# Four paddings in SBUF that shift the operands of the large matmuls to multiples of 512 bytes

## The chip, the cores and the metric

The kernel runs on one core of one Trainium2 chip. The metric is device time in microseconds (us) of one execution; the runs of a kernel are given as a median.

## The reference, cut to what matters

One layer of an encoder over 512 tokens of 1024 channels, all in float32:

```python
h = rms_norm(x, norm_mix_pre)
za, zb, q, k, v, su, sv, gl = split(h @ w_in)            # 1024 x 10240
a = silu(layer_norm(depthwise_conv(za * sigmoid(zb))))   # 31 taps
y_a = a @ w_proj_conv
o = rms_norm(diff_attention(q, k, v)) * (1 - lam_init)   # 8 heads, two softmaxes each
y_b = o @ w_proj_attn
y_c = spatial_gating(gelu(su), layer_norm(gelu(sv))) @ w_proj_sgu
g_a, g_b, g_c = split(sigmoid(gl + b_gate))
x = x + rms_norm((g_a * y_a + g_b * y_b + g_c * y_c) @ w_out)
f = square(relu(rms_norm(x) @ w_ffn_up)) @ w_ffn_down    # 1024 x 4096, 4096 x 1024
out = x + rms_norm(f)
```

## The kernel before, in words

**The products.** Every large product is made in float32r from split operands: each side has a high part (`hh`, `w_hi`, `bh`, ...) and a low part (`hl`, `w_lo`, `bl`, ...), and `mm3` (L221) issues three matmuls per K-tile of 128, high x high, low x high and high x low, into one PSUM bank. All go through `pe.matmul` at L57, all transposes through L61, both kept in the order of the program; so the trace has one line for all matmuls and they are told apart by their tiles.

```python
def mm3(o, s, m, first, last):                              # L221
    pe.matmul(o, s[0], m[0], start=first, stop=False)
    pe.matmul(o, s[0], m[1], start=False, stop=False)
    pe.matmul(o, s[1], m[0], start=False, stop=last)
```

A matmul has a stationary operand, 128 columns (512 bytes per partition) loaded by an LDWEIGHTS of its own before each matmul, and a moving operand, 512 columns (2048 bytes) or 256. A *unit* (`unit_gen`, L227) is one weight tile of 128 columns against all of K = 1024 and all 512 tokens: 24 matmuls, weights stationary, tokens moving. In this form are the units on h (the GLU's za and zb, q, k, su, the gates gl: 61 of them with 512 columns at a time; three more are done in halves of 256 columns at the start, beside the norm of x), the three branches' projections (8 units each) and the projection up (32 units, the first four with one half of 256 columns in advance). In the other form, token tile stationary and 512 columns of weights moving, are sv (192 matmuls, `sv_half`), w_out (192, `out_mm`) and the projection down (768, `down_mm`); v has it with 256 columns (384 matmuls). The attention adds scores (128), products with v (96) and transposes.

**Weights.** `load_to` (L134) loads each 512 KB weight tile by a DMA on SP's queue into `w_raw`, ScalarE rounds it to `w_hi` (L145) and VectorE takes the rest to `w_lo` (L146); three buffers of each. Five tiles, from the second half of w_out on (`xp`, L122), go into buffers of the pool `p4`.

**Other engines.** VectorE also has the 8 x 31 taps of the depthwise conv (L325), as work of low priority behind the GLU and the branches, and the conv branch's norm starts with transposes of `apad` on TensorE.

**Where tiles lie.** SBUF is handed out by pools that stand on each other like a stack, each tile rounded up to 32 bytes per partition; a pool closed gives its place to the next one. The order is: a descriptor area of 16,384 bytes and four constants of 32; `wp` with nine weight buffers of 4096; `cp` (ident, 512 bytes, and 18 small tiles); `hp` with hh and hl of 16,384 each; `cq` with the small parameters (3680 bytes); `cvp` with apad (17,344) and acc (2048); `mixp` with mix (16,384); then, one after the other, `att`, or `brp` (bh, bl) with `sgu`, `p3` or `p4` on it. The MLP's pool `fp` (gpo, 4096; fh and fl, 65,536 each) starts where cq did. Summed up, the addresses' residues modulo 512 are:

| tiles | address of the first | residue |
|---|---|---|
| w_raw, w_hi, w_lo | 16,512 | 128 |
| hh, hl, also h2h, h2l | 54,464 | 192 |
| conv buffer apad | 90,912 | 288 |
| attention's operands; bh, bl (also sh, sl, mh, ml); gvh, gvl, ch, cl | 126,688 and up | 224 |
| w_hi, w_lo in p4 | 167,648 and up | 224 |
| fh, fl | 91,328, 156,864 | 192 |

Within a tile the operands begin at multiples of 512 bytes.

Of the kernel before, what the change touches and what calls it, by code (L numbers as in the profile page):

```python
# [8 lines left out]
F32 = mybir.dt.float32  # L9
# [4 lines left out]
PSUM = bass.MemoryType.PSUM  # L14
DRAM = bass.MemoryType.DRAM

P = 128
# [11 lines left out]
SCALE = 64 ** -0.5  # L29
# A head whose sum of squares leaves float32's range has the norm factor 0, as 1 / sqrt(inf).  # L30
# The squares are summed at a scale of 2^-40, so that the sum itself stays finite.
BIG = 2.0 ** 64
# How the work is laid beside each other: the GLU's channel tiles of each head, the units ahead of the
# first head, the taps behind a GLU tile, the gate at which the conv branch's norm starts, the places at
# which the token tiles of the second norm are turned, the load of x behind which the first weights go, and
# how far behind the taps stand.
LATE = {1: [2], 3: [3], 5: [4], 6: [5], 7: [6, 7]}
# [10 lines left out]
def encoder_layer(ctx: ExitStack, tc: tile.TileContext, a: dict, out: bass.AP):  # L48
# [3 lines left out]
    class pe:  # L52
        """The tensor engine, in the order of the program."""

# [8 lines left out]
    def mk(name, bufs=1, **kw):  # L63
        return tc.tile_pool(name=name, bufs=bufs, reuse_waits="tile", **kw)
# [7 lines left out]

    # ------------------------------------------------------------ weights
    x = a["x"]
# [6 lines left out]
    def rows(n, k0, c0):  # L81
        return wv[n][:, k0:k0 + 2, c0:c0 + 512]
# [4 lines left out]
    specs = []  # L87
    # channel tiles of the GLU that wait for the attention, whose softmax leaves the tensor engine time
    late = {h: [] for h in range(H)}
# [37 lines left out]
    for nh in range(2):  # L127
        specs += [rows("w_ffn_down", k, nh * 512) for k in range(0, FT, 2)]

    wp = ctx.enter_context(mk("wp"))  # L130
    loaded = []
# [17 lines left out]
    def take(m=1, ahead=2):  # L149
        i = taken[0]  # L150
        taken[0] += m
        load_to(i + m + ahead)
        return loaded[i:i + m]

    # ------------------------------------------------------------ constants
    cp = ctx.enter_context(mk("cp"))
    hp = ctx.enter_context(mk("hp"))
    ps = {"pool": None, "a": 4, "b": 4}

    def banks(stack, na):  # L160
        """PSUM's eight banks: na for "a", the others for "b", until the stack closes."""
        ps.update(pool=stack.enter_context(mk(f"ps{na}", space=PSUM)), a=na, b=8 - na)
# [11 lines left out]
    big = ExitStack()  # L174
# [9 lines left out]
    def eps_with(p, ss, scale):  # L184
        """eps and the part of the mean square that is there already."""
        e = p.tile([P, 1], F32, tag="rs_e", bufs=4, name="rs_e")
        vec.tensor_scalar(e, ss, scale, EPS, op0=ALU.mult, op1=ALU.add)
        return e

    def rstd_of(p, ss, scale, eps=EPS, eps_tile=None, n=1, steps=1):  # L190
        """(ss * scale + eps) ** -0.5: ScalarE's root, then Newton steps to float32's accuracy."""
        v = p.tile([P, n], F32, tag=f"rs_v{n}", bufs=4 if n == 1 else 1, name="rs_v")
        vec.tensor_scalar(v, ss, scale, eps, op0=ALU.mult, op1=ALU.add)
        s = p.tile([P, n], F32, tag=f"rs_s{n}", bufs=4 if n == 1 else 1, name="rs_s")
        act.activation(s, ss, AF.Sqrt, bias=eps_t if eps_tile is None else eps_tile, scale=scale)
        r = p.tile([P, n], F32, tag=f"rs_r{n}", bufs=4 if n == 1 else 1, name="rs_r")
        vec.reciprocal(r, s)
        for _ in range(steps):
            if n == 1:
                vec.scalar_tensor_tensor(s, v, r, r, op0=ALU.mult, op1=ALU.mult)  # L200
            else:
                vec.tensor_tensor(s, v, r, op=ALU.mult)
                vec.tensor_tensor(s, s, r, op=ALU.mult)
            vec.tensor_scalar(s, s, -0.5, 1.5, op0=ALU.mult, op1=ALU.add)
            vec.tensor_tensor(r, r, s, op=ALU.mult)
        return r
# [14 lines left out]
    def mm3(o, s, m, first, last):  # L221
        """o += s^T @ m from the parts of both: three passes, what lies under float32's last bit left out."""
        pe.matmul(o, s[0], m[0], start=first, stop=False)
        pe.matmul(o, s[0], m[1], start=False, stop=False)
        pe.matmul(o, s[1], m[0], start=False, stop=last)

    def unit_gen(b, w, mov, tk=slice(0, S)):  # L227
        """b[c, tok] = W[:, c]^T @ mov, all of K = 1024."""
        for kt in range(KT):
            mm3(b, [t[:, kt] for t in w], [t[:, kt, tk] for t in mov], kt == 0, kt == KT - 1)  # L230
            yield
# [7 lines left out]

    # ------------------------------------------------------------ h = rms_norm(x), transposed  # L240
    hh = hp.tile([P, KT, S], F32R, tag="hh", name="hh")
    hl = hp.tile([P, KT, S], F32R, tag="hl", name="hl")
    with mk("p0") as p0:
# [25 lines left out]

        # the first units run on half of the tokens while the others are normalized  # L270
        hT = (hh, hl)
        norm_x(0)
        norm_x(1)
        first = take(3, 0)
# [7 lines left out]

        # small parameters: one column per block of 128 channels
        rowsrc = [("conv_b", 8), ("conv_ln_g", 8), ("conv_ln_b", 8), ("b_gate", 24), ("subln_g", 1), ("sgu_b", 8)]
# [11 lines left out]
        b = bank("b")  # L296
# [12 lines left out]

    # ------------------------------------------------------------ conv branch: GLU, then taps in the background  # L310
    cvp = big.enter_context(mk("cvp"))
    apad = cvp.tile([P, KT, S + 2 * PAD], F32, tag="apad", name="apad")
    pool.memset(apad[:, :, 0:PAD], 0.0)
    pool.memset(apad[:, :, PAD + S:], 0.0)
    mixp = big.enter_context(mk("mixp"))

# [12 lines left out]
    taps = conv_taps()  # L329

    def conv(n, behind):
        """The next n taps, behind an instruction of VectorE: work that fills its time there."""
        with tc.issue_after(behind.ins):
            keep = tc.cur_priority
            tc.cur_priority = keep + LOWP
            for _ in range(n):
                next(taps, None)
            tc.cur_priority = keep + (tc.cur_priority - keep - LOWP)
# [24 lines left out]
    b = bank("a")  # L363
# [4 lines left out]

    # -lambda
    lam2 = []  # L370
# [13 lines left out]

    # ------------------------------------------------------------ differential attention
    dist = ap_.tile([P, 896], F32, tag="dist", bufs=2, name="dist")
# [10 lines left out]
    def proj_qk(h, got):  # L397
        """q (times -1/8) and k of one head, both of its maps, as what two passes of K = 128 need:
        [qh; qh], [ql; ql] against [kh; kl], whose products are all four of the parts'."""
        wq, wk = take(2)  # L400
        bq = bank("a")
        yield from unit_gen(bq, wq, hT)
        qh = ap_.tile([P, 2, S], F32R, tag="qh", bufs=2, name="qh")
        ql = ap_.tile([P, 2, S], F32R, tag="ql", bufs=2, name="ql")
# [33 lines left out]
    def head(h, got):  # L438
        """One head of differential attention; yields where the tensor engine would wait."""
        qh, ql, kk = got["qk", h]  # L440
# [42 lines left out]
        b = bank("b")  # L483
# [6 lines left out]
        b = bank("b")  # L490
# [13 lines left out]
    run(proj_qk(0, got))  # L504
    # beside each head's softmax: the next head's q and k, and the next pair's v or a channel tile of the GLU
    fills, quota = [], []
    for h in range(H):
        n = 0
# [33 lines left out]

    # ------------------------------------------------------------ gmlp: v half, gelu and layer norm
    sg_g = bcast(sp, "sg_g", a["sgu_ln_g"], D)
# [16 lines left out]

    # ------------------------------------------------------------ attention: rms over each head, back to channels
    oss2 = oss.rearrange("p t h -> p (t h)")
# [7 lines left out]
    for h in range(H):  # L571
        next(fill)
        next(fill)
        b = bank("a")
# [29 lines left out]

    # ------------------------------------------------------------ gate and merge one branch
    mix = mixp.tile([P, KT, S], F32, tag="mix", name="mix")
# [30 lines left out]

    # ------------------------------------------------------------ spatial gating
    ws_t = {}
# [31 lines left out]
    for g in range(KT):  # L671
        (w,) = take(1)
        gc = slice(g * P, (g + 1) * P)
        b = bank("b")
# [14 lines left out]

    # ------------------------------------------------------------ conv branch: layer norm, silu  # L690
    c3 = ExitStack()
# [39 lines left out]

    # ------------------------------------------------------------ w_out, residual, second norm
    dp = ctx.enter_context(mk("dp", space=DRAM))
# [3 lines left out]
    with mk("p4") as p4:  # L737
# [21 lines left out]
        for t in range(TT):  # L759
# [4 lines left out]
            ss = p4.tile([P, 2], F32, tag="ss", bufs=4, name="ss")  # L764
# [23 lines left out]

    # ------------------------------------------------------------ squared-relu MLP
    fp = ctx.enter_context(mk("fp"))  # L790
# [3 lines left out]
    for n in range(FT):  # L794
        if n < len(early):
            b = eb[n]
            run(unit_gen(b[:, 256:512], early[n], h2, slice(256, 512)))
        else:
            (w,) = take(1)
            b = bank("a")  # L800
# [16 lines left out]
    ss = cp.tile([P, TT, 2], F32, tag="fss", name="fss")  # L817
# [58 lines left out]
```

## Time and profile before

| | us |
|---|---|
| runs of the kernel, median (lowest to highest) | 1106.67 (1105.45 to 1106.84) |
| profiled execution, span from its first to its last instruction | 1102.8 |
| TensorE busy in it | 1081.2 |
| VectorE, ScalarE busy in it | 706.2, 497.6 |

The runs' times are those of whole executions, and the span is that of the one that was profiled, without what lies ahead of its first instruction and behind its last; the runs' median is 3.9 us more than the span, and no other time is listed for the profiled execution. Times in the trace are counted from the start of the span. A matmul's busy time in the trace is longer than the distance to the start of the next, because matmuls are pipelined and their ends are modelled.

### The profile page before, as it was taken

What the parts mean: (1) busy time and instruction counts of PE and PEld (TensorE: products, weight loads), DVE (VectorE), ACT (ScalarE), POOL (GpSimd) and SP (SyncE); (2) the same over time, 40 slices, a digit from 0 to 9 for tenths busy, and PEclk for the clock granted to TensorE, in tenths of its full rate; (3) what the DMA queues carried; (4) which work ended last, traced back from release to release, by engine and by line L of the source; (5) the groups of instructions that cost most, each with busy time, mean ns of one, the idle gap of its engine ahead of it and who ended that gap; (6) DMA issues with size and microseconds to landing.
All of it is one profiled execution on the core that took longest, in us unless ns stands there. A gap on an engine that the chain in (4) does not pass through costs nothing.

```text
span 1102.8 us, 13477 instructions
## 1 busy us (share of the span) xinstructions
PE 1081.2 (98%) x5201; PEld 897.4 (81%) x5201; DVE 706.2 (64%) x1200; ACT 497.6 (45%) x800; POOL 14.0 (1%) x32
## 2 busy tenths in 40 slices
PE   5999999999999999999999999999999999999997
PEld 4989898988878888888888888889888888888885
DVE  5686878979995888997995564485444443223224
ACT  5356667777644832443222953354333332112111
POOL 3000000000000000000000000000000000000000
PEclk9999999999999999999999999999999999999999
DMA  7242333233323333223333132832333334222222
GB/s 220 78 122 74 93 96 86 68 107 85 96 78 95 115 95 94 79 78 94 96 96 96 45 109 97 267 126 86 97 97 97 96 103 164 94 93 96 96 77 77
DMA packets 149439, 111.78 MB, mean 101 GB/s; under 512 B 3957, under 2 KB 130977, under 8 KB 149376
## 3 DMA queue, kind: packets, MB, share of 16 engines
q1 hardware_dynamic: 146368, 101.73, 30.7%
q0 software_dynamic: 2288, 7.63, 2.0%
q10 hardware_dynamic: 720, 1.57, 0.4%
q8 instruction: 41, 0.67, 0.3%
q14 instruction: 22, 0.18, 0.1%
HBM read 102.52 MB, written 4.19 MB: 97 GB/s over the span
## 4 chain that ended last, share of the span: by engine, by line
PE 94%; DVE 2%; ACT 2%; DMA 1%; issue 0%; SPq 0%; DVEq 0%; ACTq 0%
PE ps_a L57 74%; PE ps_b L57 17%; PE ps_b L61 3%; DMA w_raw<-in_w_in_dram 1%; ACT y L704 0%; DVE jk L778 0%; DVE w_lo L146 0%; PE ps_a L61 0%; ACT jk L776 0%; SPq L251 0%; ACT w_hi L145 0%; DVE wk L773 0%; DVE st L589 0%; DVE h2l L218 0%; DVE wk L772 0%
## 5 line engine op out<-in xcount | busy, mean ns | idle before, releaser
L145 ACT ACTIVATE w_hi<-w_raw 128x1024 fp32r<-128x1024 f32 x176 | 186.4, 1059 | 405.2 <-PE ps_a L57 308.5
L146 DVE TENSOR_TENSOR w_lo<-w_raw,w_hi 128x1024 fp32r<-128x1024 f32 x176 | 215.1, 1223 | 228.2 <-ACT w_hi L145 227.6
L57 PE MATMUL ps_a<-hh,w_hi 128*128 128x512 f32 (+1 forms) x536 | 209.1, 390 | 0.2 <-ACT hh L217 0.2
L57 PE MATMUL ps_a<-hl,w_hi 128*128 128x512 f32 (+1 forms) x536 | 206.7, 386 | 0.3 <-DVE hl L218 0.3
L57 PE MATMUL ps_a<-hh,w_lo 128*128 128x512 f32 (+1 forms) x536 | 205.6, 384 | 0.0
L325 DVE SCALAR_TENSOR_TENSOR acc<-apad,convw,acc 128x512 f32<-128x512 f32 x232 | 173.6, 748 | 5.1
L57 PEld LDWEIGHTS ps_a<-hh,w_lo 128*128 128x128 f32 x536 | 102.1, 191 | 20.6
L57 PEld LDWEIGHTS ps_a<-hh,w_hi 128*128 128x128 f32 x536 | 102.4, 191 | 20.1 <-ACT hh L217 0.6
L57 PEld LDWEIGHTS ps_a<-hl,w_hi 128*128 128x128 f32 x536 | 102.3, 191 | 19.4 <-DVE hl L218 0.6
L57 PE MATMUL ps_a<-h2h,w_hi 128*128 128x512 f32 (+1 forms) x288 | 106.3, 369 | 0.0
L57 PE MATMUL ps_a<-h2h,w_lo 128*128 128x512 f32 (+1 forms) x288 | 105.7, 367 | 0.0
L57 PE MATMUL ps_a<-h2l,w_hi 128*128 128x512 f32 (+1 forms) x288 | 105.0, 364 | 0.0
L57 PEld LDWEIGHTS ps_a<-h2h,w_lo 128*128 128x128 f32 x288 | 54.0, 188 | 9.8
L57 PEld LDWEIGHTS ps_a<-h2l,w_hi 128*128 128x128 f32 x288 | 54.1, 188 | 9.6 <-DVE h2l L218 0.2
L57 PEld LDWEIGHTS ps_a<-h2h,w_hi 128*128 128x128 f32 x288 | 54.1, 188 | 8.4
L57 PE MATMUL ps_a<-w_hi,fl 128*128 128x512 f32 x128 | 50.4, 394 | 0.0
L57 PE MATMUL ps_b<-w_hi,fl 128*128 128x512 f32 x128 | 50.4, 394 | 0.0
L57 PE MATMUL ps_a<-w_hi,fh 128*128 128x512 f32 x128 | 50.4, 394 | 0.0
L57 PE MATMUL ps_a<-w_lo,fh 128*128 128x512 f32 x128 | 50.4, 394 | 0.0
L57 PE MATMUL ps_b<-w_hi,fh 128*128 128x512 f32 x128 | 50.4, 394 | 0.0
L57 PE MATMUL ps_b<-w_lo,fh 128*128 128x512 f32 x128 | 50.4, 394 | 0.0
L57 PE MATMUL ps_a<-w_hi,hh 128*128 128x256 f32 (+1 forms) x160 | 49.2, 308 | 0.0
(240 smaller groups left out, 1808.8 us busy)
## 6 DMA issues: line engine op xcount, KB each, us to landing
w_raw<-in_w_in_dram SPq DMA_DIRECT2D x80, 512.0 KB, 3.6
w_raw<-in_w_ffn_up_dram SPq DMA_DIRECT2D x32, 512.0 KB, 4.0
w_raw<-in_w_ffn_down_dram SPq DMA_DIRECT2D x32, 512.0 KB, 3.5
w_raw<-in_w_proj_attn_dram SPq DMA_DIRECT2D x8, 512.0 KB, 3.9
w_raw<-in_w_proj_sgu_dram SPq DMA_DIRECT2D x8, 512.0 KB, 3.8
w_raw<-in_w_proj_conv_dram SPq DMA_DIRECT2D x8, 512.0 KB, 4.0
w_raw<-in_w_out_dram SPq DMA_DIRECT2D x8, 512.0 KB, 3.5
xx<-in_x_dram SPq DMA_DIRECT2D x4, 512.0 KB, 7.6
```

What stands on the lines that cost most here:

```text
L57: return tc.keep_in_program_order(nc.tensor.matmul(*args, **kw))
L61: return tc.keep_in_program_order(nc.tensor.transpose(*args, **kw))
L145: act.activation(hi, raw, AF.Copy)
L146: vec.tensor_tensor(lo, raw, f32(hi[:, :]), op=ALU.subtract)
L325: vec.scalar_tensor_tensor(o, apad[:, c, j:j + S], convw[:, c, j:j + 1], acc, op0=ALU.mult, op1=ALU.add)
```

## The change

Four tiles are allocated that no instruction writes or reads: 384 bytes per partition ahead of `wp` (L130), 448 between `cp` and `hp` (L157), 416 ahead of `cvp` (L311), 64 ahead of `mixp` (L315). The diff, cut to its core (the rest of it drops comments and docstrings, no other code):

```diff
+    def pad(stack, name, n):
+
+        stack.enter_context(mk(name)).tile([P, n // 4], F32, tag=name, name=name)
+
+    pad(ctx, "pad0", 384)
     wp = ctx.enter_context(mk("wp"))
...
     cp = ctx.enter_context(mk("cp"))
+    pad(ctx, "pad1", 448)
     hp = ctx.enter_context(mk("hp"))
...
+    pad(big, "pad2", 416)
     cvp = big.enter_context(mk("cvp"))
...
+    pad(big, "pad3", 64)
     mixp = big.enter_context(mk("mixp"))
```

## Rows read from the trace of the kernel before

**Rows 1.** The page: the span; busy us, share and instructions of each engine.

```profile
span 1102.8 us, 13477 instructions
...
PE 1081.2 (98%) x5201; PEld 897.4 (81%) x5201; DVE 706.2 (64%) x1200; ACT 497.6 (45%) x800; POOL 14.0 (1%) x32
```

**Rows 2.** Chain of waits in order of time: start us, us, what; whole span.

```profile
315.25 22.39 PE ps_a L57 x96
...
363.53 77.72 PE ps_a L57 x336
...
500.43 5.51 PE ps_a L57 x24
...
713.97 14.96 PE ps_b L57 x66
```

**Rows 3.** The same view from 764 us on.

```profile
763.86 152.67 PE ps_a L57 x667
916.53 89.59 PE ps_b L57 x384
1006.12 89.62 PE ps_a L57 x384
```

**Rows 4.** Timeline of PE, first half of w_out: start us, us, what.

```profile
699.75 0.39 PE L57 MATMUL ps_a<-w_hi,mh 128*128 128x512 f32 x1
...
701.86 0.40 PE L57 MATMUL ps_a<-w_hi,mh 128*128 128x512 f32 x1
```

**Rows 5.** The same, second half of w_out.

```profile
724.69 0.39 PE L57 MATMUL ps_b<-w_hi,mh 128*128 128x512 f32 x1
...
726.95 0.39 PE L57 MATMUL ps_b<-w_lo,mh 128*128 128x512 f32 x1
```

**Rows 6.** Stretches: busy us (count) of each engine, granted clock, DMA share, GB/s.

```profile
core 0: us, PE busy (x) PEld busy (x) DVE busy (x) ACT busy (x) POOL busy (x), PEclk, DMA share, GB/s
22.60:25.90 3.30, 3.30 (x18) 3.30 (x16) 2.49 (x5) 1.22 (x3) 1.17 (x3) 0.50 0.07 24
...
400.00:500.00 100.00, 100.00 (x454) 81.78 (x453) 90.34 (x119) 33.87 (x44) 0.00 (x0) 1.00 0.31 90
692.00:713.50 21.50, 21.50 (x93) 17.30 (x92) 9.98 (x10) 8.06 (x9) 1.58 (x3) 1.00 0.84 281
714.50:728.50 14.00, 14.00 (x63) 11.62 (x62) 10.55 (x29) 8.10 (x18) 0.00 (x0) 1.00 0.61 186
918.00:1004.00 86.00, 86.00 (x370) 68.95 (x369) 20.62 (x21) 17.41 (x21) 0.00 (x0) 1.00 0.33 117
```

**Rows 7.** Timeline of PE, units on h, 256 columns: two rows at either clock.

```profile
24.05 0.41 PE L57 MATMUL ps_a<-hh,w_hi 128*128 128x256 f32 x1
...
25.54 0.41 PE L57 MATMUL ps_a<-hl,w_hi 128*128 128x256 f32 x1
...
26.08 0.28 PE L57 MATMUL ps_a<-hl,w_hi 128*128 128x256 f32 x1
...
27.26 0.28 PE L57 MATMUL ps_a<-hh,w_lo 128*128 128x256 f32 x1
```

**Rows 8.** Timeline of PE in the attention: v with 256 columns, then four transposes.

```profile
149.83 0.28 PE L57 MATMUL ps_a<-w_lo,hh 128*128 128x256 f32 x1
...
152.33 0.28 PE L57 MATMUL ps_a<-w_hi,hl 128*128 128x256 f32 x1
152.44 0.60 PE L61 MATMUL ps_b<-ident,at 128*128 128x128 f32 x4
152.80 0.37 PE L57 MATMUL ps_a<-w_hi,hh 128*128 128x256 f32 x1
```

**Rows 9.** Instructions on apad, 560 to 640 us: duration ns, first and last start.

```profile
L61 PE MATMUL ps_b<-ident,apad x32: 270/272/273, 606.0 to 614.9; 128*128 128x128 f32 x32
...
L325 DVE SCALAR_TENSOR_TENSOR apad<-apad,convw,acc x1: 749/749/749, 591.6 to 591.6; 128x512 f32<-128x512 f32 x1
```

## The prediction

> **What bounds the kernel now.** Read the page's busy table first: TensorE (PE) is busy 1081.2 of 1102.8 us, VectorE (DVE) 706.2 [rows 1]. Little time is spent waiting for anything, so the question is how fast TensorE goes while it works. Busy time can't say that, since the end of a matmul is modelled and lies behind the start of the next; the distance of the starts can. Next read the chain of waits in order of time: a piece "PE ps_a L57 x24" is 24 matmuls one behind the other, and its length over its count is their distance. A unit on h takes 5.51 us for 24, that is 229.6 ns each, the first half of the v part of the gMLP 22.39 / 96 = 233.2, and 66 matmuls of the second half of w_out 14.96 / 66 = 226.7 [rows 2]. A stretch of 336 matmuls in 77.72 us is half units on h and half products with w_proj_attn; with 168 x 229.6 = 38.6 us off, the latter take 39.1 / 168 = 233.0 [rows 2]. The projection up has 152.67 / 667 = 228.9, the projection down 89.59 / 384 = 233.3 in its first half and 233.4 in its second [rows 3]. All of these are fp32r matmuls with 512 columns.
>
> So the distance goes by stage. Set beside it the residues of the two operands' addresses (modulo 512 bytes, table above). The clean pair is w_out. Its first half reads the weights at residue 128 against tokens at 224: the starts of matmuls nine apart give (701.86 - 699.75) / 9 = 234.4 ns [rows 4]. Its second half reads weights from the second pool at 224 against the same tokens: (726.95 - 724.69) / 10 = 226 ns [rows 5], over the longer piece 226.7. Same operation, same shape, same line; what differs is the address of the weights, the PSUM tag and the load of the DMA queues. The tag is not it: the projection down has 233.3 in ps_b and 233.4 in ps_a [rows 3]. Nor the DMA: the two halves have a DMA share of 0.84 and 0.61, but the projection down, at 0.33, is as slow as the first [rows 6]. That leaves the address: equal residues gave the shortest distance.
>
> **What the change removes, adds and moves.** It adds no instruction: a padding is a tile that nobody writes or reads. It moves addresses. Weights go from residue 128 to 128 + 384 = 512, that is 0. The constants' pool ends 64 past a multiple, so 64 + 448 = 512 puts h there. The pool cq ends 96 past, and 96 + 416 = 512 puts the conv pool there; that pool ends 448 past, and 448 + 64 = 512 puts mix, and behind it everything of the attention, the branches and the second weights' pool, at residue 0. The MLP's pool starts where cq does, so fh and fl go from 192 to 0. Every operand of a large product is then at residue 0, and both operands are at equal residues, as in w_out's second half.
>
> The price of a 512-column matmul at (0, 0) is in no row. From above it is bounded by the slowest row, 234.4 [rows 4]. From below by one column per cycle: at the granted clock of 0.50 (the 1.2 GHz level) [rows 6] 256-column matmuls begin (25.54 - 24.05) / 7 = 213 ns apart [rows 7], which is 256 / 1.2 with nothing on top, so at 2.4 GHz 512 columns take no less than 213.3. I take 226.7, the row with equal residues, since that is what the change makes everywhere. For 256 columns the rows have 118.0 with tokens at 192 against weights at 128, (27.26 - 26.08) / 10 [rows 7], and 113.6 the other way round, (152.33 - 149.83) / 22 [rows 8]; 113.6 is half of 226.7 to 0.3 ns, so I take it for all of them.
>
> The sum, by products and their counts in the code:
> - projection down: 768 x (233.3 - 226.7) = 5.1 us
> - units on h (13 of the GLU, 16 of q and k, 8 of u, 24 gates; 61 x 24 = 1464): 1464 x 2.9 = 4.2
> - the three branches' projections: 24 x 24 = 576, x 6.3 = 3.6
> - projection up behind its first four units: 28 x 24 = 672, x 2.2 = 1.5
> - v part of the gMLP: 192 x 6.5 = 1.2
> - first half of w_out: 96 x 7.7 = 0.7
> - 192 of 256 columns at the start of the projection up: x 4.4 = 0.8
> - nothing for the second half of w_out, the scores, the products with v and the spatial product, whose operands have equal residues now (224, 224); nothing for the 384 of 256 columns that make v, at 113.6; nothing for the first 144, which lie beside the norm of x; nothing for the transposes, four of which take 152.80 - 152.44 = 0.36 us [rows 8] and whose operand `ident` merely goes from residue 128 to 0; if they gained or lost a tenth, some 370 of them would move the sum by 3 us.
>
> Together 17.1 us. The span goes from 1102.8 to 1085.7. The median of the runs is 3.9 us above the span; that stays, and 1106.67 - 17.1 = **1089.6 us**.
>
> What covers the gain: VectorE is the next engine. In the stretch from 400 to 500 us it is busy 90.3 of 100 us [rows 6], where the forecast takes 2 us off. Its conv taps end at 591.6 + 0.75 = 592.4 us, and the transposes that need them start at 606.0 [rows 9]: 13.6 us of slack, of which 1.2 + 2.4 + 3.7 = 7.3 us go (v part, two branches, most units on h). Weights, ScalarE and the DMAs have more room. One edge moves: since the tiles of the start don't shift with those behind the paddings, a sigmoid's output will lie over cw too and wait for eight more transposes, at most 0.7 us by [rows 8], on ScalarE beside a unit: nothing.
>
> **The rivals.** *More than forecast* (the floor falls too). 226.7 is still 13.4 above 213.3, and residue 224 is 32 past a multiple of 64; if that costs half of it, 4112 matmuls of 512 columns gain 6.7 more, 27.5 us: 1062; all of it would give 1035 before VectorE binds, and the slack of 13.6 us would be gone in either. For it: half clock shows no surcharge. Against it: 113.6 for 256 columns with both operands at multiples of 64 [rows 8] has the same surcharge. Beside this stands a rule of the Trainium skill (TensorE: Matmul & The Clock Gate, Back-to-back issue gap): N / 2.4 + 2.5 ns, 215.8 for 512 columns, whatever the address; by it the estimate would be 1045. No row here goes below 226.
>
> *Address is not the cause* (the paddings do nothing). Then w_out's halves differ by something that I did not see, and the time is 1106.7. For it: only one stage shows equal residues cleanly; in the attention it can't be read apart from the products woven in. Against it: two DMA loads and both PSUM tags at the same 233. The Trainium skill speaks for this rival (SBUF — State Buffer, Who interferes with whom): the moving operand and the weight load have independent read ports, so where one lies against the other should not matter. The distances of 234.4 and 226 at one shape disagree [rows 4, 5].
>
> *Only half of the products.* The 226.7 was seen with 512 columns of a weight matrix moving and tokens as the stationary side. The v part, w_out and the projection down have that form: 1.2 + 0.7 + 5.1 = 7.0 us. If products with weights as the stationary side keep their distance, 1099.7.
>
> *Slower*: at (0, 0) the two read streams, and the writes into hi and lo tiles that now begin at residue 0 too, meet in every matmul instead of some. Place: every 512-column product; price: up to the slowest row, 234.4, in place of 229.6 for the units on h (1464 x 4.8 = 7.0), 228.9 (672 x 5.5 = 3.7) and 226.7 (0.7), and 1 to 1.4 on the others (1.8): 13.2 us, 1119.9. It decides once the mean over these products, 230.9 ns now, is passed. Against it: equal residues at 224 are the best row.
>
> **How the numbers follow.** A measurement here can tell 0.2% from no change. Forecast 0.58; more 0.14; half 0.10; no effect 0.09; slower 0.09. Faster is the first three, 0.82; same 0.09; slower 0.09. The range reaches from the half price of "more", 1062, taken as 1061, to 1105: no effect and slower, 0.18 together, are left out.
>
> **What would show it.** Right: the two pieces of the projection down at 87.0 us for 384 in the chain, the unit on h at 5.44 for 24, both halves of w_out at one distance, busy times of VectorE and ScalarE as before. The forecast is wrong if (0, 0) products stay at 229 or more, or if PE waits appear before the transposes of the conv branch at about 600 us.

## The result, and the profile after

The changed kernel takes 1093.32 us (median of 4 runs, 1092.42 to 1094.24). The kernel before, run beside it, takes 1106.55 (1105.45 to 1106.84). The ratio is 0.9885, 95% interval 0.9872 to 0.9897: faster by 13.2 us. I had forecast 1089.6 and a gain of 17.1.

The page of the changed kernel first: its span, then busy us, share and count of each engine.

```profile
span 1092.2 us, 13476 instructions
...
PE 1067.4 (98%) x5201; PEld 899.2 (82%) x5201; DVE 705.5 (65%) x1200; ACT 497.4 (46%) x800; POOL 13.9 (1%) x32
```

Against [rows 1], TensorE's busy time fell by 13.8 us at the same 5201 matmuls, and VectorE's and ScalarE's stayed within 0.7. So nothing was removed; the same work passed faster. The execution behind this page lasted 1094.24 us, 2.0 more than its span. That holds for every profiled execution of the layer below, so the one of [rows 1], with 1102.8, was an execution of about 1104.8 by estimate.

The chain of waits of the changed kernel in order of time (start us, us, what) has the pieces that answer to the first three of [rows 2].

```profile
316.69 21.80 PE ps_a L57 x96
...
364.07 76.21 PE ps_a L57 x336
...
452.76 5.44 PE ps_a L57 x24
```

The same view from 764 us on answers to [rows 3].

```profile
763.96 147.11 PE ps_a L57 x649
911.07 87.04 PE ps_b L57 x384
998.11 87.05 PE ps_a L57 x384
```

In these pieces length over count is one number: 21.80 / 96 = 227.1 ns, 76.21 / 336 = 226.8, 5.44 / 24 = 226.7, 147.11 / 649 = 226.7, 87.04 / 384 = 226.7. Before, these pieces had 233.2, 231.3, 229.6, 228.9 and 233.3. The projection down alone gives 89.59 + 89.62 - 87.04 - 87.05 = 5.12 us.

The two halves of w_out on the timeline of PE (start us, us, what), which answer to [rows 4] and [rows 5]; from the first row of each pair to the second it is twelve matmuls.

```profile
695.79 0.39 PE L57 MATMUL ps_a<-w_lo,mh 128*128 128x512 f32 x1
...
698.51 0.39 PE L57 MATMUL ps_a<-w_lo,mh 128*128 128x512 f32 x1
...
717.78 0.39 PE L57 MATMUL ps_b<-w_hi,ml 128*128 128x512 f32 x1
...
720.50 0.39 PE L57 MATMUL ps_b<-w_hi,ml 128*128 128x512 f32 x1
```

2.72 / 12 = 226.7 ns in both: the difference between the halves is gone. A row's own duration, 0.39, is as before and says nothing of it.

One form got slower. The timeline of PE in the attention, where v is made with 256 columns, eight matmuls from the first row to the second, then four transposes; it answers to [rows 8].

```profile
149.76 0.28 PE L57 MATMUL ps_a<-w_hi,hh 128*128 128x256 f32 x1
...
150.72 0.28 PE L57 MATMUL ps_a<-w_hi,hl 128*128 128x256 f32 x1
150.84 0.60 PE L61 MATMUL ps_b<-ident,at 128*128 128x128 f32 x4
151.19 0.36 PE L57 MATMUL ps_a<-w_hi,hh 128*128 128x256 f32 x1
```

0.96 / 8 = 120.0 ns where it was 113.6. The four transposes take 0.35 us where they took 0.36.

Not every 512-column matmul became faster. Behind a matmul of another form (a transpose, or v with 256 columns) the distances need up to ten matmuls to settle. From the GLU's first 512-column unit on, without the distance that holds the change of form itself and without waits, the next nine are 230.1 ns on the average, as they were before (230.2); all later ones are 226.7, where they were 231.1. Two rows from the second half of the gMLP's v part, where four transposes stand ahead of every twelve matmuls, five matmuls from the one to the other, which is 230 ns each:

```profile
341.73 0.39 PE L57 MATMUL ps_b<-w_lo,hh 128*128 128x512 f32 x1
...
342.88 0.39 PE L57 MATMUL ps_b<-w_hi,hh 128*128 128x512 f32 x1
```

Where the time went, from the first and last matmul start of each stage in the two traces (the order of the matmuls is the same, so stages can be cut at the same matmul). The third column is an experiment from below, with less padding, in which the operands' residues are equal too, modulo 256.

```
stage (matmuls)                         before    after   e5_mod256
start, beside the norm of x (185)        30.40    31.62     29.98
GLU, 512 columns (24)                     5.62     5.57
first v, 256 columns (159)               25.32    25.82     25.82
attention, with more of v (1281)        243.69   243.73    243.73
v part of the gMLP (248)                 53.87    52.95
attention branch and gates (368)         84.20    82.52
gMLP's u and spatial product (272)       58.64    58.27
gMLP branch and gates (408)              94.32    92.48
conv branch's norm (160)                 29.44    29.39
conv branch and gates (240)              55.83    54.67
w_out, first half (96)                   22.49    21.76
w_out, second half (112)                 23.56    24.69     23.57
up, 256 columns at the start (208)       25.17    25.38
up, 512 columns (672)                   153.83   152.35
down, two halves (768)                  178.96   173.85
```

From the first 512-column unit to the last matmul it is 1054.95 before and 1043.43 after, 11.5 us less. Two stages took something back in waits and clock, not in the distance of matmuls.

The first is the second half of w_out, 1.1 us longer. The chain of the changed kernel from 690 to 730 us:

```profile
694.76 10.19 DMA w_raw<-in_w_out_dram
704.97 1.07 ACT w_hi L150
706.06 1.24 DVE w_lo L151
707.31 4.13 DMA w_raw<-in_w_ffn_up_dram
```

Here the chain does not run through TensorE: it follows a weight tile from its DMA, which takes 10.19 us, over the rounding on ScalarE and VectorE. The norm of the new x stands behind that rounding on VectorE, and TensorE's transposes wait 0.9 us for its result (jk, third row of the waits below). Both profiled executions of the changed kernel have this stall: 24.69 us in this one, 24.37 in e9_after_again. Two other kernels with equal distances have 25.41 (e2_no_pad0) and 23.57 (e5_mod256). Whether the layout or the execution decides it, no run shows.

The second is the start. Stretch from 20 to 27 us, busy us (count) of each engine, granted clock, DMA share, GB/s; the changed kernel's row:

```profile
20.00:27.00 7.00, 4.74 (x23) 4.77 (x24) 5.36 (x18) 3.07 (x6) 1.17 (x3) 0.51 0.46 141
```

and the same stretch of the kernel before:

```profile
20.00:27.00 7.00, 4.92 (x29) 4.95 (x30) 5.08 (x17) 2.90 (x6) 1.17 (x3) 0.76 0.34 105
```

The granted clock is 0.51 here against 0.76. 0.5 is the 1.2 GHz level, at which TensorE spent nearly all of these 7 us in the changed kernel and about half of them before. This differs between executions with the same layout: e8_fh_only, whose tiles at the start lie as in the kernel before, has 0.55 in this stretch, and its start takes 31.70 us in place of 30.40. Ahead of it TensorE waits for the norm of x, as the waits of the changed kernel's PE show (what was waited for: us in total, times, longest us):

```profile
PE ps_b L61 <- DVE rs_r L203: 9.7, 1, 9.7
PE ps_b L61 <- DVE rs_s L210: 4.5, 1, 4.5
PE ps_b L61 <- DVE jk L786: 1.2, 2, 0.9
```

The first two lie at the start and were 10.0 and 2.3 before; of the third, 0.9 us is the stall in w_out. No wait appears ahead of the conv branch's transposes. They start at 602.7, the last taps end at 588.6 + 0.75 = 589.4 us, so 13.3 of the 13.6 us of slack [rows 9] are left.

### The profile page after: what moved, and what is told of

It is laid out like the page before. It is cut to its first block, busy times and chain, and to the rows that moved or that the text cites. A ratio compares the mean times of both kernels' runs of the same rounds, so it can differ in the third digit from the quotient of the medians.

```text
span 1092.2 us, 13476 instructions
## 1 busy us (share of the span) xinstructions
PE 1067.4 (98%) x5201; PEld 899.2 (82%) x5201; DVE 705.5 (65%) x1200; ACT 497.4 (46%) x800; POOL 13.9 (1%) x32
## 4 chain that ended last, share of the span: by engine, by line
PE 91%; DVE 3%; DMA 2%; ACT 2%; issue 1%; SPq 0%; DVEq 0%; ACTq 0%
PE ps_a L57 72%; PE ps_b L57 15%; PE ps_b L61 3%; DMA w_raw<-in_w_in_dram 1%; DMA w_raw<-in_w_out_dram 1%; DVE w_lo L151 1%; ACT w_hi L150 1%; DVE jk L786 0%; ACT jk L784 0%; ACT y L712 0%; DVE wk L780 0%; DMA w_raw<-in_w_ffn_up_dram 0%; DVE wk L781 0%; PE ps_a L61 0%; SPq L257 0%
## 5 line engine op out<-in xcount | busy, mean ns | idle before, releaser
L57 PE MATMUL ps_a<-hl,w_hi 128*128 128x512 f32 (+1 forms) x536 | 204.3, 381 | 0.5 <-DVE hl L224 0.5
```

The source lines that it names most:

```text
L57: return tc.keep_in_program_order(nc.tensor.matmul(*args, **kw))
```

## The experiments

**Theory 1** is the one that the prediction took: what counts is where the moving operand begins relative to the stationary one. Its main rival is that the multiple of 512 itself counts, as the change is described. "Difference" below is the moving operand's address less the stationary one's, in bytes per partition. The first and the fourth kernel hold nothing but groups of matmuls on one weight tile and compute nothing of the layer.

### e1_map: the distance as a function of both residues

The groups run through eight residues (steps of 64) of either operand, and some multiples of 32, at 512 and at 256 columns:

```python
for m, s in PAIRS + ODD:
    for k in range(count):
        mo, so = m // 4 + (k % 6) * 512, s // 4 + (k % 12) * 128
        nc.tensor.matmul(o[:, 0:cols], sta[:, so:so + P], mov[:, mo:mo + cols], ...)
```

> This kernel leaves the whole layer out: it only issues groups of fp32r matmuls on fixed operands, for every pair of residues (moving, stationary) modulo 512 in steps of 64 bytes and some in steps of 32, first with 512 columns (12 per pair), then with 256 (24 per pair). Theory 1, the difference of the two residues counts: every pair with moving = stationary has 226.7 ns with 512 columns and 120 with 256; moving - stationary = -64 has 233 and 113.4, +64 has 229 and 118, whatever the residues themselves. Theory 2, starting at a multiple of 512 counts: (0, 0) has 226.7, pairs such as (64, 64) or (128, 128) have 229 to 234. Theory 3, it is the neighbours in the layer (other engines' accesses): no pair differs, all at one distance.

Mean distance of starts in the second half of each group, by difference modulo 256 (all at a granted clock of 1.00; the pair (0, 0) at 512 columns fell into the start and is left out):

```
difference          0              64              128             192
512 columns   226.7 (14 of 15   228.8 to 229.0   232.5 to 232.7   233.3
              pairs; one 230.8)
256 columns   120.0 to 120.3   117.8            118.2 to 118.8   117.8 (12 pairs),
                                                                 113.3 (4)
```

Differences that are multiples of 32 but not of 64 have 233.0 to 234.3 at 512 columns, as w_out's first half has (128 against 224, [rows 4]). At 512 columns the pairs with one difference agree, whether the residues are 0, 64 or 192; and (0, 256) has the same 226.7 as (192, 192). The exceptions had not settled: the distances of a group with equal residues begin at 228 to 236 and reach 226 to 227 after one to ten matmuls, and (256, 0), with 230.8, gets there only with its last two. Of three equal pairs at odd multiples of 32, (224, 224) has 226.7, (32, 32) 228.3 and (96, 96) 230.8, in groups that begin in the same way. So the difference counts, not the residue, and with a period of 256 bytes, not 512. The distances of the kernel before can be read off: units on h have difference 192 - 128 = 64 (228.8 to 229.0; 229.6 in [rows 2]), the projection down 128 - 192, that is 192 (233.3; 233.3 in [rows 3]). At 256 columns equality is the worst of these four, not the best, and the pairs of difference 192 do not agree: 12 of 16 have 117.8, where theory 1 expected 113.4.

### e2_no_pad0: equal residues that are not 0

```diff
-    pad(ctx, "pad0", 384)
```

All that lies behind moves down by 384 bytes, so every operand of a large product lies at residue 128.

> The changed kernel without its first padding of 384 bytes: weights, h, the branches' operands and fh, fl all lie at residue 128, so equal but no multiple of 512. Theory 1 (difference counts): as the changed kernel, 1093 us, units on h at 5.45 us for 24, projection down at 87.0 us for 384, v's matmuls of 256 columns at 120 ns. Theory 2 (multiples of 512 count): back toward the kernel before, 1104 to 1107 us, projection down at 89.6.

1095.04 us (1094.60 to 1095.18), ratio 0.9902 (0.9884 to 0.9920). The end of its chain:

```profile
912.04 87.04 PE ps_b L57 x384
999.08 87.05 PE ps_a L57 x384
```

The same 226.7 ns without one operand at a multiple of 512. The rival falls. v has 120.0 ns here too. Of the 1.7 us above the changed kernel's median, the traces put 0.7 into the second half of w_out (25.41 against 24.69).

### e3_pad0_only: the weights at 512, the differences as before

```diff
     pad(ctx, "pad0", 384)
...
-    pad(ctx, "pad1", 448)
...
-    pad(big, "pad2", 416)
...
-    pad(big, "pad3", 64)
```

> The first padding alone: the weights lie at residue 0, h, fh and fl at 64, the branches' operands at 96; every difference between two operands is that of the kernel before. Theory 1: as the kernel before, 1106.5 us, projection down at 89.6 us for 384, v's matmuls of 256 columns at 113.4 ns. Theory 2: a part of the gain, since one operand of each product lies at a multiple of 512: 1098 to 1103 us.

1105.28 us (10 runs, 1104.19 to 1106.30), ratio 0.9993 (0.9984 to 1.0002): no difference. The end of its chain:

```profile
917.04 89.60 PE ps_b L57 x384
1006.64 89.61 PE ps_a L57 x384
```

Every stage from the first 512-column unit on is within 0.01 us of the kernel before, and v has 113.7 ns on the average, as before. Shifting everything by one padding does nothing; it is the paddings between the operands that act.

### e4_map2: what the spread hangs on

Groups with difference 0, 64, 128 and 192, with 128, 64 and 32 stationary columns in fp32r, and with bf16 operands; then 256-column groups behind different groups.

> This kernel leaves the whole layer out: groups of matmuls on fixed operands at differences (moving minus stationary) of 0, 64, 128 and 192 bytes; fp32r with 128, 64 and 32 stationary columns, bf16 with 128, and groups of 256 columns entered from two different neighbours. Theory 1a, the read of the moving operand collides with the read of the next weights: with 32 stationary columns, a quarter of the weight bytes, the spread over the differences (227 to 233.5 ns at 128 columns) shrinks to a quarter, under 2 ns; in bf16, at half the bytes, there is no spread. Theory 1b, the spread belongs to the pair of start addresses and not to the bytes read: 227 to 233.5 at every width and in bf16 too. For the groups of 256 columns with a difference of -64: 113.4 ns if the difference alone counts; 113.4 behind one neighbour and 117.8 behind the other if the state in which the stream is entered counts.

```
                     difference   0      64     128    192
512 columns  fp32r, 128 wide     226.6  228.8  232.5  233.3
             fp32r,  64 wide     230.0  228.0  229.3  232.5
             fp32r,  32 wide     231.9  231.7  231.1  231.8
             bf16,  128 wide     215.8  215.8  215.8  215.9
256 columns  fp32r, 128 wide     120.0  117.7  118.6  113.3
             fp32r,  64 wide     113.3  116.7  116.7  118.9
             fp32r,  32 wide     113.3  113.3  113.3  113.3
             bf16,  128 wide     109.2  109.1  109.2  109.1
```

(Difference 0 at 512 columns and 128 wide is from the later groups of this kernel; the first fell into the start.) The effect of the address needs fp32r and a wide stationary operand: with 32 columns or with bf16 it is gone. With 64 columns there is a spread, but equal addresses are not the best case (230.0 against 228.0 at 64). That fits theory 1a as far as the spread goes, two reads of four-byte operands that get into each other's way, though no run shows the reads themselves; and with 32 columns the distance settles near the slow end at 512 columns and at the fast end at 256, which a mere meeting of reads does not give. What remains, 226.7 - 213.3 = 13.4 ns over one column per cycle, is not explained.

The 256-column groups of difference 192 (that is -64) showed two distances: 117.8 each time behind a 512-column group, 113.3 in three of four cases behind a 256-column group of difference 0. Same addresses, same instructions: a stream of 256-column matmuls keeps one of two rhythms, and what ran before it counts.

### e5_mod256: the period, in the layer

```diff
-    pad(ctx, "pad0", 384)
+    pad(ctx, "pad0", 128)
...
-    pad(ctx, "pad1", 448)
+    pad(ctx, "pad1", 192)
...
-    pad(big, "pad2", 416)
+    pad(big, "pad2", 160)
```

> Paddings of 128, 192, 160 and 64 bytes: the weights and the branches' operands lie at residue 256, h, fh and fl at 0, so most pairs differ by 256 modulo 512 and are equal modulo 256. If the period is 256 bytes: as the changed kernel, 1093 to 1095 us, projection down 87.0 us for 384, v's matmuls at 120 ns. If it is 512 (equal residues modulo 512 are needed): h, the projections up and down and the v part of the gMLP lose their gain, 1103 to 1107 us, projection down 89.6.

1093.52 us (1091.86 to 1094.02), ratio 0.9895 (0.9878 to 0.9911), as the change. The end of its chain:

```profile
908.62 87.04 PE ps_b L57 x384
995.66 87.05 PE ps_a L57 x384
```

544 bytes of padding do what 1312 do. This execution had no stall in w_out, and from the first 512-column unit to the last matmul it took 1042.28 us, 12.7 less than before.

### e6_diff128: a difference of 128

```diff
-    pad(ctx, "pad1", 448)
+    pad(ctx, "pad1", 64)
```

Weights at residue 0, h and all that lies behind it at 128.

> Paddings of 384, 64, 416 and 64 bytes: weights at residue 0 and everything else at 128, so that the difference is +128 or -128 for all large products except the second half of w_out. If the difference sets the distance as in the map (233.3 ns at 128): units on h and projection up lose 2136 x 4 ns = 8.5 us and v's matmuls (118.6 ns) 384 x 5.2 = 2.0 against the kernel before, 1115 to 1117 us; projection up 2.33 us per 10 matmuls, projection down 89.6 us for 384. If the paddings help in another way than by the difference: no slower than before, 1095 to 1106.

1112.97 us (1110.55 to 1113.49), ratio 1.0065 (1.0048 to 1.0081): slower. The end of its chain:

```profile
922.89 89.23 PE ps_b L57 x384
1012.13 89.23 PE ps_a L57 x384
```

89.23 / 384 = 232.4 ns, what e1_map has for difference 128. The projection up with 512 columns takes 156.16 us (672 x 232.4), where it took 153.83. All operands lie at multiples of 128, and still it is slower than the kernel before: alignment is not what helps. It came out 2 to 4 us under what I expected, because I had priced the difference 128 at 233.3 ns, which is the map's value for 192: at 232.4 the 2136 matmuls lose 1.9 us less, and the projection down gains 0.7. From the first 512-column unit to the last matmul the trace has 1062.54 us, 7.6 more than before, and the median is 7.3 us longer. The profiled execution was the shortest of the four, 1110.55; its start was at full clock and took 28.32 us, 2.1 less than before.

### e8_fh_only: one term of the sum alone

The kernel before, with one line:

```diff
+    ctx.enter_context(mk("padf")).tile([P, 48], F32, tag="padf", name="padf")
     fp = ctx.enter_context(mk("fp"))
```

192 bytes put fh and fl at residue 128 modulo 256, as the weights are.

> The kernel before with one padding of 192 bytes, ahead of the MLP's pool: fh and fl go from residue 192 to 384, which is equal modulo 256 to the weights' 128; nothing else moves. Theory 1 with the period of 256: the projection down goes from 89.6 to 87.0 us for 384, every other stage stays, 5.1 us less in all: ratio 0.9954. Theory 2 (multiples of 512): no change, ratio 1.000.

1101.24 us (1100.57 to 1101.50), ratio 0.9959 (0.9946 to 0.9973); 4.5 us of the run's 1105.69. The end of its chain:

```profile
918.13 87.06 PE ps_b L57 x384
1005.20 87.05 PE ps_a L57 x384
```

The projection down gives 5.1 us in the trace, and no other stage from the first 512-column unit on moves by more than 0.15. Of the 12.6 us that all of the change is worth by the traces (below), this one padding has 40%.

### e7_v_shift, e9_after_again and e10_v_shift_again: v at another difference

In e7 and e10 the first three paddings are none, 192 and 160; each `w_hi` and `w_lo` gets 256 bytes more, and the two weight tiles of each v begin 192 bytes in. For place, five small tiles (lq1, lk1, lq2, lk2, lpr) move from `cq` to the attention's pool; the diff, cut:

```diff
+    shifted = set()
...
+        shifted.update((len(specs), len(specs) + 1))
...
-            hi = p.tile([P, 1024], F32R, tag="hi", bufs=n_, name="w_hi")
+            e = 64 if p is wp else 0
+            o = 48 if len(loaded) in shifted else 0
+            hi = p.tile([P, 1024 + e], F32R, tag="hi", bufs=n_, name="w_hi")[:, o:o + 1024]
...
-        pr = cq.tile([P, 64], F32, tag="lpr", name="lpr")
+        pr = ap_.tile([P, 64], F32, tag="lpr", name="lpr")
```

e9 is the changed kernel without an edit, beside e10 on one chip.

> An attempt at a faster version: all operands at equal residues modulo 256 (no first padding, then 192, 160 and 64 bytes), weight buffers of 4352 bytes, and the weight tiles of v written 192 bytes further in, so that v's matmuls of 256 columns have a difference of -64 as in the kernel before. If the difference alone sets their distance: 384 x (120 - 113.4) = 2.5 us under the changed kernel, 1090 to 1092 us. If their 113.4 ns hung on the neighbours in the kernel before (the map has 117.8 for most such pairs): 0.8 us or nothing.

> The changed kernel once more, unchanged, beside the others on one chip: 1092 to 1094 us. Its stages from the first 512-column unit on take the same as in the first profile; the first 185 matmuls and the second half of w_out may differ by 1 to 3 us from run to run.

> The version with v's weights 192 bytes further in, once more, beside the changed kernel. If only v's 384 matmuls count, which took 116.3 ns in place of 120 in its first profile: 384 x 3.7 = 1.4 us less than the changed kernel. If its 2.4 us came from the start of the run and the second half of w_out, which differ between executions: 0 to 1 us less.

e7: 1090.90 us (1089.09 to 1092.36), ratio 0.9868 (0.9852 to 0.9885). e9: 1093.95 (1090.54 to 1095.41), 0.9890 (0.9873 to 0.9908). e10: 1089.93 (1089.17 to 1091.60), 0.9861 (0.9847 to 0.9874). The timeline of e10's PE in v, eleven matmuls from the first row to the second:

```profile
146.04 0.28 PE L57 MATMUL ps_a<-w_hi,hh 128*128 128x256 f32 x1
...
147.29 0.28 PE L57 MATMUL ps_a<-w_hi,hl 128*128 128x256 f32 x1
```

1.25 / 11 = 113.6 ns in this stretch, and 117.8 in others: over all of v the mean of e7 is 116.4, between the two rhythms. So of the 2.5 us that the expectation put on v, the stages with v gave 0.23 + 0.61 = 0.84 us against the changed kernel. The rest of the difference of 4 us between e9 and e10, which is more than either expectation of e10 allowed, is not v's. e10's stretch from 20 to 27 us (columns as above):

```profile
20.00:27.00 7.00, 5.66 (x49) 5.69 (x50) 4.46 (x7) 2.17 (x4) 3.41 (x7) 1.00 0.63 97
```

and its chain in w_out:

```profile
689.82 14.96 PE ps_a L57 x66
704.78 14.96 PE ps_b L57 x66
```

The clock is 1.00 where the changed kernel had 0.51, which with the waits there makes the start 3.4 us shorter (28.24 against 31.62), and the chain in w_out runs through TensorE, as in [rows 2], with a stall of 0.3 us left (23.82 us against 24.69). The same tiles have moved in memory, so a cause in the layout can't be excluded for these two; e6_diff128, with v's tiles not shifted, had the full clock too. Each execution is recorded with its mean granted clock, and executions of equal clock are closer: at 0.998 they took 1089.09 (e7) and 1089.17 (e10) against 1090.54 (e9), at 0.997 1090.76, 1091.04 (e7) and 1091.60 (e10) against 1092.42 and 1092.65 (the changed kernel's first runs), some 1.4 us apart on these few executions. The intervals of e9 and e10 just touch. The version is the fastest that was run, by 4.0 us over the change in the medians; 0.84 of that is accounted for by its edit, and most of the rest goes with the clock.

## Why the prediction was right, and where it was off

**The floor of 226.7 ns** was right, and so was the reason, but for the period: equal residues modulo 256 are enough (e5_mod256). I took it from w_out's second half [rows 2, 5] for all products with 512 columns. It holds to 0.1 ns in every stream of one form, from about the tenth matmul on, and e1_map, e3_pad0_only, e6_diff128 and e8_fh_only show that the difference of addresses makes it. Why equal addresses are the fastest, no run shows.

**The terms.** Projection down: 5.1 forecast, 5.12 measured. Projection up behind its first units: 1.5, and 153.83 - 152.35 = 1.48. First half of w_out: 0.7, and 0.73. A unit on h: 5.51 - 5.44 = 0.07 us by the chain, 2.9 x 24 as forecast. The stages from the v part of the gMLP to the conv branch hold 1.2 + 3.6 of v part and branches and, with 8 units for u and 24 for the gates, 768 x 2.9 = 2.2 of the units on h: 7.0 forecast, and 0.92 + 1.68 + 0.37 + 1.84 + 0.05 + 1.16 = 6.0 measured. The attention branch and the gMLP branch came out as forecast. The missing 1.0 lies in the v part (0.4), u and the spatial product (0.3), the conv branch's norm (0.2) and the conv branch (0.2). In the first three, transposes stand between the products. The matmuls right behind them gained less than the price that the sum took: in the v part's second half they have 230.7 ns, not 226.7. Further behind, the units on h of u and of the conv branch's norm had 228.7 before, not 229.6. In the conv branch TensorE stops twice, for 0.1 us each.

**The step that failed** is "113.6 is half of 226.7 to 0.3 ns, so I take it for all of them". Two rows with 256 columns gave 118.0 and 113.6 [rows 7, 8], and I explained them by the rule that held for 512. There it is false: at equal residues 256 columns take 120.0, the slowest value of e1_map. So v, which I costed at nothing, lost 2.1 us: its 384 distances add up to 47.00 us, where they had 44.85. The 29 units of the GLU, q and k, which lie between v, scores and transposes, gained 1.2 of their 2.0, and the scores and the products with v, put at nothing, gained 0.5. From the first 512-column unit to the end of the attention the changed kernel is 0.5 us behind, where the forecast had it 2.0 ahead. The 0.8 us for the 256-column units at the start of the projection up came out as a loss of 0.2. So the sum is 2.5 + 1.0 too high where 256-column matmuls stand, mostly by this step, and with the 1.0 above 17.1 becomes 12.6. The traces have 11.5 + 1.1 (the stall in w_out) = 12.6; the medians have 13.2, with starts that differ between executions.

**What stays for the median.** "The median of the runs is 3.9 us above the span; that stays" mixed two things: 2.0 us lie outside the span in every profiled execution, and the other 1.9 say that the profiled execution was a faster one than the median's.

**The cover.** VectorE's taps kept 13.3 us of slack, the transposes their time, and the sigmoid's new wait shows nowhere.

**The rivals.** *More than forecast*: no stage of a kernel of the layer and no group with 128 stationary columns goes below 226.6 on the average at 512 columns in fp32r. The rule that spoke for it, the Trainium skill's TensorE: Matmul & The Clock Gate, Back-to-back issue gap (N / 2.4 + 2.5 ns, 215.8 for 512 columns, there given for an isolated matmul), agrees with the bf16 groups to the digit, 215.8, and is 11 to 18 ns short for fp32r. *Address is not the cause* fell with e2, e3 and e6. The Trainium skill's SBUF — State Buffer, Who interferes with whom, which spoke for it (independent read ports for the moving operand and the weight load), agrees with bf16, where no difference of addresses changes anything; the conclusion that I drew from it, that addresses do not matter, is contradicted in fp32r by 226.7 against 233.3. *Only half of the products* is refuted by the units on h at 5.44 us. *Slower*: residue 0 is as good as residue 128 (e2), and to be slower, as e6 is, the residues of the two operands have to differ.

## What to carry to other kernels

In an fp32r kernel that TensorE bounds, look at the distance of matmul starts by product, not at busy times, and set beside it the addresses of both operands: with 512 columns moving and 128 stationary they should be equal modulo 256 bytes per partition, and a few tiles' paddings are enough. Count the gain only for streams of one form: here the nine matmuls behind a change of form gained nothing on the average. A price read at one shape is not to be halved for half the columns; here the best case of one shape was the worst of the other. Alignment to a power of two is only a way to make addresses equal: operands at multiples of 128 that differed by 128 lost 0.65%.

## What the runs showed of the hardware that I had not expected

- At full clock the distance of fp32r matmuls with 512 columns and 128 stationary columns goes with the operands' difference modulo 256 bytes: 226.7, 228.8, 232.5, 233.3 ns at 0, 64, 128, 192. With 64 stationary columns the order is another one (230.0, 228.0, 229.3, 232.5), with 32 it is 231 to 232 throughout, in bf16 215.8 throughout.
- Behind a matmul of another form that distance needs up to ten matmuls to reach 226.7 ns; the nine behind the change of form have 230.1 on the average in the changed kernel.
- At the 1.2 GHz level there is no surcharge to see: 213 ns for 256 columns [rows 7], against 113.3 to 120 at the full clock, where one column per cycle would be 106.7.
- A stream of 256-column fp32r matmuls has two stable distances at the same addresses, 113.3 and 117.8, depending on what ran ahead of it (e4_map2). Why, no run tells.
- After TensorE's first matmuls and its wait for the norm of x the granted clock of the stretch from 20 to 27 us is 1.00, 0.76, or 0.51 to 0.57, depending on the execution, and the start takes 28.0 to 28.3, 30.0 to 30.8, or 31.4 to 31.7 us with it. What decides it was not tried. It is as large as many of the terms of the sum, so a change of 3 us in one profile of this kernel proves nothing until the stage that holds it is named.
